# Decoder trunk on one core: one TensorE pass per gate entry issued in two pieces

## Chip, core and metric

The kernel runs on 1 core of one Trainium2 chip. The metric is the device time of the whole program in microseconds (us); lower is better.

## What is computed

The reference is a trunk of two layers (D_MODEL 1024, 256 tokens, D_FF 2816), each of three sub-layers: a SwiGLU feed-forward network (FFN), a token mixer, and a second FFN. So the program holds four FFNs, and the change touches only these.

```python
def swiglu(x, w_gate, w_up, w_down):
    return (jax.nn.silu(x @ w_gate) * (x @ w_up)) @ w_down
...
for l in range(DEPTH):
    f1 = swiglu(rms_norm(h, ffn1_pre_g[l]), ffn1_w_gate[l], ffn1_w_up[l], ffn1_w_down[l])
    h = h + 0.5 * rms_norm(f1, ffn1_post_g[l])
    m = token_mixer(rms_norm(h, mix_pre_g[l]), ...)
    h = h + rms_norm(m, mix_post_g[l])
    f2 = swiglu(rms_norm(h, ffn2_pre_g[l]), ffn2_w_gate[l], ffn2_w_up[l], ffn2_w_down[l])
    h = h + 0.5 * rms_norm(f2, ffn2_post_g[l])
```

## The kernel before

Every large product is done with each operand split into a high part and a low part (`fp32r`): three TensorE passes, high x high, high x low and low x high, add up in the same PSUM bank. A *pass* below is one `pe.matmul`; each comes with its own load of a 128 x 128 stationary operand (LDWEIGHTS, the engine row PEld), also where two passes in a row use the same one.

The 2816 hidden columns of an FFN are worked in 11 chunks of 256 (`NC` = 11; in the order strings they are 0 to 9 and A). Chunks 0 and 1 go by rows of tokens (`gu_rows`, passes of 512 columns). For chunks 2 to A, `gu_cols` computes the gate (step `G`, tile qg) and the up projection (step `U`, tile qu) with the hidden columns on the partitions: two halves `b` of 128 hidden columns, each 8 slices of K x 3 passes, so 48 passes of 256 columns (all 256 tokens) for one step. The stationary operand is a slice of the weight unit, the moving one is `xT`, the transposed tokens. `evac_cols` (step `E`) turns the two PSUM banks into the hidden tile `hT` on VectorE and ScalarE. `down` (steps `D`, c and token tile t) adds that chunk into four PSUM banks (facc): 2 token tiles x 2 halves of 512 output columns x 2 slices of K x 3 passes through `mm3` (L253, L254, L255), so 24 passes of 512 columns for the two steps of a chunk.

The order of TensorE's work is written out by hand:

```python
FFN_START = "g00 g10 sc0 xb1 u00 u10 e0 g01 g11 sc1 u01 u11 e1"
FFN_BODY = "G2 t0 rsb U2 t1 E2 side D00 D01 D10 D11 G3 U3 E3 D20 D21"
FFN_END = "D80 D90 DA0 fa0 D81 D91 fb0 xb0 DA1 fa1 fb1"
...
for c in range(4, NC):
    order += [f"{n}{c:X}" for n in "GUE"]
    if c < NC - 2:
        order += [f"D{c - 1:X}0", f"D{c - 1:X}1"]
```

So after G2 and U2, between which transposes stand (`t0`, `rsb`, `t1`: tiles ht and rsB), the steps run G3 U3 D2 G4 U4 D3 G5 U5 D4 G6 U6 D5 G7 U7 D6 G8 U8 D7 G9 U9 GA UA, then the downs of 8, 9 and A. Group c is entered through `down(1)` for c = 3, and through `down(c - 2)` for c = 4 to 9; group A follows U9 with no down step between. Weights stream from memory on SP's queue (`fetch`), are split by ScalarE (L229) and VectorE (L230) into ring units (`prepare`), and a unit is given back by `done` after the last pass that reads it.

Of the kernel before, what the change touches and what calls it, by code (L numbers as in the profile page):

```python
# [21 lines left out]
KD = D // P  # L22
S = 256
NT = S // P
# [20 lines left out]
FFN_BODY = "G2 t0 rsb U2 t1 E2 side D00 D01 D10 D11 G3 U3 E3 D20 D21"  # L45
FFN_END = "D80 D90 DA0 fa0 D81 D91 fb0 xb0 DA1 fa1 fb1"
NC = FF // 256

C_ID = 0
C_TRI = 128  # L50
# [36 lines left out]
def trunk(ctx: ExitStack, tc: tile.TileContext, T, out):  # L87
    nc = tc.nc
    pe, act, dve, pool = nc.tensor, nc.scalar, nc.vector, nc.gpsimd
# [13 lines left out]
    def bank(name):  # L103
        return psp.tile([P, 512], F32, tag="bank", name=name)

    def acc_tile(name):
        return [bank(name) for _ in range(2)]
# [13 lines left out]
    xT = big.tile([P, 2, KD, NT, P], F32R, name="xT")  # L121
# [18 lines left out]
    def cols_unit(key, W, k0, nk, c0, ncol):  # L140
        src = W[k0 * P:(k0 + nk) * P, c0:c0 + ncol].rearrange("(k p) c -> p k c", p=P)
        spec(key, [(0, P, nk, ncol, src)])

    def ffn_specs(l, f):
        wg, wu, wd = (T[f"ffn{f}_w_{n}"][l] for n in ("gate", "up", "down"))

        def gu(nm, c):
            cols_unit((l, f, nm, c), wg if nm == "g" else wu, 0, KD, c * 256, 256)

        def dn(c):  # L150
            cols_unit((l, f, "d", c), wd, 2 * c, 2, 0, D)

        for nm in "gu":
            for h in range(2):
                cols_unit((l, f, nm, h), wg if nm == "g" else wu, 4 * h, 4, 0, 512)
        for c in range(2, NC):
            gu("g", c)
            gu("u", c)
            if c == 2:
                dn(0)  # L160
                dn(1)
            elif c < NC - 1:
                dn(c - 1)
        dn(NC - 2)
        dn(NC - 1)

# [78 lines left out]
    def done(key, raw_only=False):  # L245
        del units[key]
        st["raw" if raw_only else "live"] -= 1
        pump()

    def mm3(o, pairs, first, last):  # L250
        n = len(pairs)
        for i, (sh, sl, mh, ml) in enumerate(pairs):
            pe.matmul(o, sh, mh, start=first and i == 0, stop=False)  # L253
            pe.matmul(o, sh, ml, start=False, stop=False)  # L254
            pe.matmul(o, sl, mh, start=False, stop=last and i == n - 1)  # L255


    def rstd(srcs, name, scale, eps=None):
# [70 lines left out]
    def ffn(l, f, rs, finish, side=None):  # L329
# [11 lines left out]
        def gu_rows(nm, h, t):  # L341
            if h == 0:
                ps[nm, t] = bank("p" + nm)
            u = units[l, f, nm, h]
            mm3(ps[nm, t], [(xT[:, 0, 4 * h + k, t, :], xT[:, 1, 4 * h + k, t, :], u[:, 0, k, :], u[:, 1, k, :])
                            for k in range(4)], h == 0, h == 1)
            if t == 1:
                done((l, f, nm, h))
# [24 lines left out]
        def gu_cols(nm, c):  # L373
            o = bank("q" + nm)
            u = units[l, f, nm, c]
            for b in range(2):
                bs = slice(b * P, (b + 1) * P)
                o3 = o[:, b * 256:(b + 1) * 256].rearrange("p (t n) -> p t n", t=NT)
                n = 0
                for k in range(KD):  # L380
                    for a, h in ((0, 0), (0, 1), (1, 0)):
                        pe.matmul(o3, u[:, a, k, bs], xT[:, h, k], start=n == 0, stop=n == 3 * KD - 1)  # L382
                        n += 1
            ps[nm] = o
            done((l, f, nm, c))
# [14 lines left out]
        def down(c, t):  # L400
            if acc[t] is None:
                acc[t] = acc_tile("facc")
            u = units[l, f, "d", c]
            if c < 2:
                q = [[hT[t][:, a, (2 * c + k) * P:(2 * c + k + 1) * P] for k in range(2)] for a in range(2)]
            else:
                q = [[hT["c", c][:, a, k * 256 + t * P:k * 256 + (t + 1) * P] for k in range(2)] for a in range(2)]
            for j, js in enumerate(HALF):
                mm3(acc[t][j], [(q[0][k], q[1][k], u[:, 0, k, js], u[:, 1, k, js]) for k in range(2)],
                    c == 0, c == NC - 1)  # L410
            if t == 1:
                done((l, f, "d", c))

        order = (FFN_FIRST if side else FFN_START).split() + FFN_BODY.split()
        for c in range(4, NC):
            order += [f"{n}{c:X}" for n in "GUE"]
# [3 lines left out]
        for n in order:  # L420
            if n == "rsb":
                tmp["rsB"] = broadcast_rows(rs)
            elif n == "side":
                if side:
                    side()
            elif n[:2] == "fa":
                finish[0](int(n[2]), acc[int(n[2])], ev[int(n[2])])
            elif n[:2] == "fb":
                finish[1](int(n[2]))
            elif n[:2] == "sc":  # L430
                scales(int(n[2]))
            elif n[:2] == "xb":
                if n[2] == "1" or not finish[2]:
                    pre_b(int(n[2]))
            elif n[0] in "gu":
                gu_rows(n[0], int(n[1]), int(n[2]))
            elif n[0] == "e":
                evac_rows(int(n[1]))
            elif n[0] == "t":
                tr(int(n[1]))  # L440
            elif n[0] in "GU":
                gu_cols(n[0].lower(), int(n[1], 16))
            elif n[0] == "E":
                evac_cols(int(n[1], 16))
            else:
                down(int(n[1], 16), int(n[2]))
# [85 lines left out]
    def mixer(l, rs, finish):  # L532
# [15 lines left out]
        def proj(nm, t):  # L548
            if nm == "kw":
                kwps[t] = o = bank("kw")[:, :280]  # L550
            else:
                accs[nm, t] = o = bank(nm)
            for h in range(2):
                u = units[l, nm, h]
                mm3(o, [(xT[:, 0, 4 * h + k, t, :], xT[:, 1, 4 * h + k, t, :], u[:, 0, k, :], u[:, 1, k, :])
                        for k in range(4)], h == 0, h == 1)
                if t == 1:
                    done((l, nm, h))
# [461 lines left out]
```

## Time and profile before

| | |
|---|---|
| median of 2 runs | 979.79 us (979.56 to 980.02) |
| profiled execution, whole time | 977.4 us |
| its span, first to last instruction | 975.4 us |
| TensorE passes / weight loads | 6294 / 6294 |
| TensorE busy | 956.4 us, 98% of the span |

The whole time of the profiled execution is 2.0 us above its span, and 2.4 us below the median. Busy time of TensorE overlaps from pass to pass, because a pass is shown from its start until its last result is written; the pace of a stream of passes is read from the distance of starts, or from the chain of work, which gives each pass only the time until the next one.

### The profile page before, as it was taken

To read this page: it belongs to the slowest core of one execution; us is meant where nothing else is said; L and a number is where in the kernel's file an instruction comes from. 1 tells how busy PE (TensorE), PEld (TensorE's weight loads), DVE (VectorE), ACT (ScalarE), POOL (GpSimd) and SP (SyncE) were. 2 spreads that over 40 slices of the span, in tenths; PEclk is the share of its full clock that TensorE was granted. 3 is DMA by queue.
4 is the path that set the end of the run, shared out by engine and by line. 5 is a ranking of instruction groups with operands and counts; after the bars stand their busy time and mean duration, and the time that the engine had idled before them with its cause. 6 is when DMAs were issued, how large, how long until landed. Compare 5 with 4: busy or idle time off the path is not lost.

```text
span 975.4 us, 15327 instructions
## 1 busy us (share of the span) xinstructions
PE 956.4 (98%) x6294; PEld 857.2 (88%) x6294; DVE 646.5 (66%) x864; ACT 478.7 (49%) x760; POOL 81.3 (8%) x136
## 2 busy tenths in 40 slices
PE   6999999999999999999999999999999999999997
PEld 5999999988778999999989999998887789999996
DVE  5785565678988655565677565567699777565552
ACT  5663443457557543443455443445468464443431
POOL 2000000030034000000030000003101320000000
PEclk9999999999999999999999999999999999999999
DMA  8876565457526555565557565653773167655611
GB/s 294 304 250 192 191 196 175 151 178 172 169 76 214 199 192 174 191 196 175 171 178 254 190 197 177 191 196 113 196 194 107 44 204 249 197 191 176 195 63 43
DMA packets 123294, 175.99 MB, mean 180 GB/s; under 512 B 13092, under 2 KB 95320, under 8 KB 123224
## 3 DMA queue, kind: packets, MB, share of 16 engines
q1 hardware_dynamic: 122936, 174.43, 56.1%
q8 instruction: 49, 0.80, 0.3%
q10 hardware_dynamic: 288, 0.59, 0.2%
q14 instruction: 21, 0.17, 0.1%
HBM read 173.95 MB, written 1.05 MB: 179 GB/s over the span
## 4 chain that ended last, share of the span: by engine, by line
PE 95%; DVE 2%; ACT 1%; DMA 1%; issue 0%; DVEq 0%; POOLq 0%; ACTq 0%; POOL 0%
PE qg L382 21%; PE qu L382 21%; PE facc L253 8%; PE facc L255 8%; PE facc L254 8%; PE oacc L253 2%; PE pu L255 2%; PE pu L253 2%; PE pg L254 1%; PE oacc L255 1%; PE pu L254 1%; PE oacc L254 1%; PE pg L255 1%; PE pg L253 1%; PE yT L767 1%; PE chp L795 1%
## 5 line engine op out<-in xcount | busy, mean ns | idle before, releaser
L229 ACT ACTIVATE unit<-raw 128x1024 fp32r<-128x1024 f32 (+2 forms) x320 | 322.5, 1033 | 348.0 <-issue 291.7
L230 DVE TENSOR_TENSOR unit<-raw,unit 128x1024 fp32r<-128x1024 f32 (+2 forms) x320 | 375.8, 1195 | 135.1 <-ACT unit L229 134.8
L382 PEld LDWEIGHTS qg<-xT,unit 128*128 128x128 f32 x1728 | 207.6, 189 | 2.5
L382 PE MATMUL qu<-xT,unit 128*128 128x256 f32 x1728 | 208.9, 281 | 0.0
L382 PE MATMUL qg<-xT,unit 128*128 128x256 f32 x1728 | 208.6, 280 | 0.0
L382 PEld LDWEIGHTS qu<-xT,unit 128*128 128x128 f32 x1728 | 205.4, 189 | 0.0
L253 PE MATMUL facc<-unit,hT 128*128 128x512 f32 x352 | 137.7, 391 | 0.0
L255 PE MATMUL facc<-unit,hT 128*128 128x512 f32 x352 | 137.0, 389 | 0.0
L254 PE MATMUL facc<-unit,hT 128*128 128x512 f32 x352 | 136.9, 389 | 0.0
L255 PEld LDWEIGHTS facc<-unit,hT 128*128 128x128 f32 x352 | 66.1, 188 | 13.8
L254 PEld LDWEIGHTS facc<-unit,hT 128*128 128x128 f32 x352 | 66.1, 188 | 12.4
L253 PEld LDWEIGHTS facc<-unit,hT 128*128 128x128 f32 x352 | 66.1, 188 | 12.4
L392 DVE TENSOR_TENSOR gp<-qg,rsB 128x512 f32<-128x512 f32 x36 | 24.8, 690 | 64.3 <-PE qg L382 64.3
L269 POOL TENSOR_TENSOR mspost<-ev,s 128x1 f32<-128x1 f32 x8 | 4.7, 592 | 664.2 <-ACT sq L263 664.2
L397 DVE SCALAR_TENSOR_TENSOR h<-qu,m 128x512 f32<-128x512 f32 x36 | 24.9, 691 | 50.8 <-PE qu L382 50.4
L394 ACT ACTIVATE m<-gp 128x512 f32<-128x512 f32 x36 | 22.3, 619 | 10.7 <-DVE gp L392 10.6
L743 ACT ACTIVATE pr<-s,mx 128x128 f32<-128x128 f32 (+1 forms) x64 | 26.1, 432 | 2.5 <-DVE mx L741 2.4
L395 DVE SCALAR_TENSOR_TENSOR m<-m,gp 128x512 f32<-128x512 f32 x36 | 24.7, 686 | 3.7 <-ACT m L394 3.7
L253 PE MATMUL pg<-unit,xT 128*128 128x512 f32 x64 | 26.0, 407 | 0.4 <-ACT unit L229 0.4
L293 DVE TENSOR_TENSOR fg<-facc,gpost 128x512 f32<-128x512 f32 x16 | 10.8, 688 | 23.5 <-ACT sq L263 23.5
L254 PE MATMUL pg<-unit,xT 128*128 128x512 f32 x64 | 25.9, 405 | 0.1
L255 PE MATMUL pg<-unit,xT 128*128 128x512 f32 x64 | 25.5, 399 | 0.0
(259 smaller groups left out, 1103.0 us busy)
## 6 DMA issues: line engine op xcount, KB each, us to landing
raw<-in_ffn_w_down_dram SPq DMA_DIRECT2D x44, 1024.0 KB, 5.0
raw<-in_ffn_w_gate_dram SPq DMA_DIRECT2D x42, 1024.0 KB, 5.4
raw<-in_ffn_w_up_dram SPq DMA_DIRECT2D x42, 1024.0 KB, 5.3
raw<-in_w_in_dram SPq DMA_DIRECT2D x14, 1024.0 KB, 5.4
raw<-in_w_out_dram SPq DMA_DIRECT2D x4, 1024.0 KB, 5.1
raw<-in_w_out_dram SPq DMA_DIRECT2D x8, 512.0 KB, 7.1
raw<-in_w_in_dram SPq DMA_DIRECT2D x4, 560.0 KB, 3.8
raw<-in_ffn_w_up_dram SPq DMA_DIRECT2D x4, 512.0 KB
```

Source lines behind the costliest of these rows:

```text
L229: act.activation(u[:, 0, i:i + step], r[:, i:i + step], AF.Copy)
L230: dve.tensor_sub(u[:, 1, i:i + step], r[:, i:i + step], u[:, 0, i:i + step].bitcast(F32))
L253: pe.matmul(o, sh, mh, start=first and i == 0, stop=False)
L254: pe.matmul(o, sh, ml, start=False, stop=False)
L255: pe.matmul(o, sl, mh, start=False, stop=last and i == n - 1)
L293: dve.tensor_mul(fg, acc[h], gpost[:, sl])
L382: pe.matmul(o3, u[:, a, k, bs], xT[:, h, k], start=n == 0, stop=n == 3 * KD - 1)
L392: dve.tensor_tensor(b2(gp), b2(g), tmp["rsB"][:, None, :].to_broadcast([P, 2, S]), op=ALU.mult)
L394: act.activation(m, gp, AF.Tanh, scale=0.5)
L395: dve.scalar_tensor_tensor(m, m, 1.0, gp, op0=ALU.add, op1=ALU.mult)
L397: dve.scalar_tensor_tensor(h, u, 0.5, m, op0=ALU.mult, op1=ALU.mult)
L743: act.activation(prs[v][:, b0 + i, :], sb[v][:, i, :], AF.Exp, bias=mx[:, i:i + 1], accum_out=cf[:, v, b0 + i:b0 + i + 1])
```

## The change

One pass next to the entry of each of the gate groups 3 to 9 is issued as two passes on column ranges of the same result, in one of three forms. For groups 3, 6 and 9 it is the first gate pass (256 columns), issued as two of 128, one for each token tile. For groups 4 and 7 it is the last pass of the down step before (512 columns, token tile 1, output half 1), issued as 256 + 256; for groups 5 and 8 the same pass as 384 + 128. The sums are the same. Nothing else moves. An FFN gets 7 more passes and weight loads, the program 28.

```diff
+ENTRY_G = (3, 6, 9)
+EXIT_D = {2: (256,), 5: (256,), 3: (384,), 6: (384,)}
...
-    def mm3(o, pairs, first, last):
+    def mm3(o, pairs, first, last, cut=()):
         n = len(pairs)
         for i, (sh, sl, mh, ml) in enumerate(pairs):
             pe.matmul(o, sh, mh, start=first and i == 0, stop=False)
             pe.matmul(o, sh, ml, start=False, stop=False)
-            pe.matmul(o, sl, mh, start=False, stop=last and i == n - 1)
+            if cut and i == n - 1:
+                for a, b in zip((0,) + cut, cut + (512,)):
+                    pe.matmul(o[:, a:b], sl, mh[:, a:b], start=False, stop=last, skip_group_check=True)
+            else:
+                pe.matmul(o, sl, mh, start=False, stop=last and i == n - 1)
...
-                        pe.matmul(o3, u[:, a, k, bs], xT[:, h, k], start=n == 0, stop=n == 3 * KD - 1)
+                        if n == 0 and b == 0 and nm == "g" and c in ENTRY_G:
+                            for t in range(NT):
+                                pe.matmul(o3[:, t], u[:, a, k, bs], xT[:, h, k, t], start=t == 0, stop=False,
+                                          skip_group_check=True)
+                        else:
+                            pe.matmul(o3, u[:, a, k, bs], xT[:, h, k], start=n == 0, stop=n == 3 * KD - 1,
+                                      skip_group_check=True)
                         n += 1
...
-                    c == 0, c == NC - 1)
+                    c == 0, c == NC - 1, EXIT_D.get(c, ()) if (t, j) == (1, 1) else ())
```

## Rows read from the trace of the kernel before

**Rows 1.** The page: busy time, granted clock by slices, chain by engine.

```profile
PE 956.4 (98%) x6294; PEld 857.2 (88%) x6294; DVE 646.5 (66%) x864; ACT 478.7 (49%) x760; POOL 81.3 (8%) x136
...
PEclk9999999999999999999999999999999999999999
...
PE 95%; DVE 2%; ACT 1%; DMA 1%; issue 0%; DVEq 0%; POOLq 0%; ACTq 0%; POOL 0%
```

**Rows 2.** Chain in order of time, group 5 (start us, us, what).

```profile
91.92 0.23 PE facc L254
92.15 0.23 PE facc L255
92.38 5.65 PE qg L382 x48
98.03 5.65 PE qu L382 x48
103.68 0.23 PE facc L253
```

**Rows 3.** Chain in order of time, group 2 of the last FFN.

```profile
806.77 0.24 PE pu L255
807.00 5.46 PE qg L382 x48
812.46 0.44 PE ht L369 x4
812.90 0.22 PE rsB L323 x2
813.12 5.46 PE qu L382 x48
818.58 0.44 PE ht L369 x4
```

**Rows 4.** Timeline inside qg, group 5, then group 2 (start, us, engine, instruction).

```profile
92.80 4.87 PE L382 MATMUL qg<-xT,unit 128*128 128x256 f32 x40
...
807.76 4.70 PE L382 MATMUL qg<-xT,unit 128*128 128x256 f32 x40
```

**Rows 5.** Groups by form inside the same two streams: busy us, mean ns.

```profile
L382 PE MATMUL qg<-xT,unit 128*128 128x256 f32 x40 | 4.9, 281 | 0.0
...
L382 PE MATMUL qg<-xT,unit 128*128 128x256 f32 x38 | 4.5, 276 | 0.0
```

**Rows 6.** Windows of group 5 (G, U, D4), then G2 of two FFNs.

```profile
core 0: us, PE busy (x) PEld busy (x) DVE busy (x) ACT busy (x) POOL busy (x), PEclk, DMA share, GB/s
92.21:97.87 5.66, 5.66 (x50) 5.65 (x49) 2.36 (x2) 2.01 (x2) 0.00 (x0) 1.00 0.70 201
97.87:103.52 5.65, 5.65 (x51) 5.65 (x49) 3.65 (x4) 2.53 (x3) 0.00 (x0) 1.00 0.64 184
103.52:108.96 5.44, 5.44 (x27) 4.51 (x25) 3.65 (x4) 2.53 (x3) 0.00 (x0) 1.00 0.46 180
514.58:520.05 5.47, 5.47 (x50) 5.47 (x49) 4.09 (x4) 2.01 (x2) 0.00 (x0) 1.00 1.01 344
806.84:812.30 5.46, 5.46 (x50) 5.46 (x48) 4.08 (x4) 2.01 (x2) 0.00 (x0) 1.00 1.04 357
```

**Rows 7.** Timeline, 24-pass streams of the two mixers, chp and chg.

```profile
251.49 3.09 PE L795 MATMUL chp<-xT,unit 128*128 128x256 f32 x24
...
257.96 3.07 PE L795 MATMUL chg<-xT,unit 128*128 128x256 f32 x24
...
730.12 3.01 PE L795 MATMUL chp<-xT,unit 128*128 128x256 f32 x24
...
736.51 2.98 PE L795 MATMUL chg<-xT,unit 128*128 128x256 f32 x24
```

**Rows 8.** Chain in order of time, group A after U9, second FFN.

```profile
457.67 5.65 PE qu L382 x48
463.32 5.65 PE qg L382 x48
468.98 5.65 PE qu L382 x48
```

**Rows 9.** Timeline of weight loads in front of short passes, second mixer.

```profile
744.04 0.98 PEld L690 LDWEIGHTS cs<-kk,qT 128*128 128x128 f32 x8
```

**Rows 10.** Window of D0 and D1 after U2, third FFN (columns as in Rows 6).

```profile
526.51:537.51 11.00, 11.00 (x51) 9.10 (x50) 6.50 (x7) 4.92 (x6) 0.00 (x0) 1.00 0.57 183
```

## The prediction

> **What bounds the kernel now.** I read the page first. TensorE is busy for 98% of the span, 95% of the chain that ended last runs through it, and the granted clock is in its top tenth in every slice, so the upper of the two levels, 2.4 GHz [rows 1]. There is no idle time to win: what counts is how long each TensorE pass takes until the next one starts. A mean over the kernel hides that, so I read the chain in order of time, stream by stream. A gate or up step of group 5 takes 5.65 us for its 48 passes, and the down passes around it 0.23 us each [rows 2]. The gate step of group 2, with the same 48 passes of the same shape, takes 5.46 us [rows 3]. This difference is the subject of the case.
>
> Inside the two streams the pace can be worked out from the timeline: (4.87 - 0.281) / 39 = 117.7 ns from start to start in group 5, and (4.70 - 0.276) / 39 = 113.4 ns in group 2 [rows 4], with the durations of one pass from the groups by form, 281 and 276 ns [rows 5]. So the same instruction has two paces, **loose** (117.7) and **tight** (113.4), and each stream keeps its own to the end. Half of the 512-column pace, 5.44 / 24 = 226.7 ns [rows 6], is 113.3 ns, so the tight pace is what the columns need and the loose one adds 4.3 ns to each pass.
>
> What decides between them? Not load from outside: the loose windows have less VectorE work and less DMA than the tight ones (DMA share 0.70 and 0.64 against 1.01 and 1.04) [rows 6]. Not shape or code line: in the mixers the same line runs 24 passes in 3.09 and 3.07 us in one layer and in 3.01 and 2.98 us in the other [rows 7]. What fits is **how the stream is entered**. Group 2's gate comes out of pu passes and its up step out of transposes: tight in all four FFNs (8 streams). Groups 3 to 9 are entered straight out of a down stream that runs at an even 226.7 ns; these gate steps, and the up steps right behind them, are all loose, and so are the gate and up steps of A, which follow U9 without a break and just keep the pace [rows 8]. That makes 8 groups x 2 steps x 4 FFNs = 64 loose streams of 48 passes, 3072 passes x 4.3 ns = 13.2 us, which is all that there is to win.
>
> **The change part by part.** The change puts a short pass into each of these 28 entries. First the cost, then what it may set off.
>
> *First gate pass as 128 + 128 (groups 3, 6, 9).* A pass can't start before its stationary operand is in. The streaming of 128 columns would take half of 113.4, 57 ns, but each piece brings a load of its own. In front of passes of 32 columns, eight such loads show a pace of (0.98 - 0.19) / 7 = 113 ns, with 0.19 us for one load [rows 9]; transposes of 128 columns run at 0.44 / 4 = 110 ns [rows 3]. No row shows an fp32r pass of 128 columns, so the cost of the extra piece lies between 0 (two pieces of 57 ns) and 118 ns (two at the loose pace in place of one). I take the load as what binds, the nearest rows: 2 x 110 - 116 = 104 ns. Twelve of them: 1.25 us, bounds 0 to 1.4.
>
> *Last down pass as 256 + 256 (groups 4, 7).* Two tight passes are 227 ns, what the whole pass takes; two loose ones are 235.4, 9 ns more. Eight of them: 0 to 0.07 us, I take 0.03.
>
> *Last down pass as 384 + 128 (groups 5, 8).* The 384 columns lie midway between 113.4 and 226.7, so 170 ns, then 110 for the piece that waits for its load: 280 - 227 = 53 ns. Eight of them: 0.42 us, bounds 0 to 0.45.
>
> All pieces lie on the path, since TensorE has no gap in which they could hide. **Sum of the costs: 1.7 us, bounds 0 to 1.9.** No DMA, no other engine's instruction and no queue is moved; the bank given to the next step and the unit given back by `done` are signalled by the last piece, at most a tenth of a us later. VectorE is busy for 2.4 to 3.7 us of a step of 5.65 us [rows 6], so it also keeps up with steps that are 0.2 us shorter.
>
> *What it may set off.* A stream that turns tight at its entry saves 5.65 - 5.46 = 0.19 us in the gate step, settling included [rows 2, 3], and 48 x 4.3 ns = 0.21 us in each step behind it that keeps the pace. That is 0.40 us for a group, and 0.82 us for the entry of group 9, which carries A too. Over four FFNs: the 128 + 128 entries (3, 6, 9) can give 4 x (0.40 + 0.40 + 0.82) = 6.5 us, the 384 + 128 entries (5, 8) 3.2 us, the 256 + 256 entries (4, 7) 3.2 us, 12.9 us in all.
>
> *What is given back.* A down stream that comes out of a tight up step may need some passes to come back to 226.7 ns. The one case of before is D0 and D1 behind U2: 11.00 us against 2 x 5.44 = 10.88 [rows 6, 10], most of which is the step out of the transposes. I take 0.03 us for each down step behind a group that turned tight, and 0 to 0.06 (passes at 229 in place of 226.7 ns) as bounds.
>
> *Which forms work?* The 128-column pieces make TensorE wait for a weight load, as nothing in the even down stream does; entries behind short passes and transposes are those that are mostly tight in before (all U2; of the four mixer streams shown, two) [rows 3, 7]. 256 + 256 leaves no such wait: the gate is then entered out of 256-column passes, and in before U entered from a loose G stays loose [rows 2, 8]. So I expect the two forms with a 128-column piece to work and 256 + 256 not to.
>
> [...]
>
> **The rivals.**
>
> A (forecast): the 20 entries with a 128-column piece turn tight, the 8 others stay loose. -6.5 - 3.2 + 1.7 + 0.6 (20 down or closing steps at 0.03) = -7.4 us, so 977.4 - 7.4 = 970.0 in a profiled execution, or 979.8 - 7.4 = 972.4 as a median (the median is 2.4 us above the profiled time).
>
> B: all 28 turn tight; any disturbance next to the entry is enough. -12.9 + 1.7 + 0.8 = -10.4, so 969.4. For it: the pu stream ahead of G2 has passes of 512 columns only, and still leads to tight [rows 3]. Against it: what is said of 256 + 256.
>
> C: only one of the forms with a 128-column piece works. 128 + 128 alone: -6.5 + 1.7 + 0.4 = -4.4, so 975.4. 384 + 128 alone: -3.2 + 1.7 + 0.2 = -1.3, so 978.5.
>
> D, on the other side (slower than before): the pace is set by something that the short pass doesn't touch, such as the operands of the stream itself, each entry falls back to 117.7 ns, and only the costs are left: +1.7, so 981.5; up to +3.6 (983.4) if 28 down steps lose their even pace as well, at 0.06 each. It decides as soon as fewer than about 5 entries turn: 1.7 us of cost over 0.40 of gain is four to five. For it: down to gate is loose in 28 of 28 cases, so this state is a strong one, and mixer streams behind short passes are loose too [rows 7].
>
> That the change doesn't do what it says would be 28 pieces that the compiler joins again, with no difference; the count of passes, 6322 in place of 6294, would tell.
>
> **How the numbers follow.** A 0.35, B 0.27, C 0.15, D 0.20, others (a costlier piece, or no pieces) 0.03. The forecast is A: 972.4, and with the costs open by about 2 us either way I keep 972.4. The range reaches from B with a part of its cost bounds (968) over A and C to D's first value (982): it leaves out the lowest part of B, the upper part of D and the others, under 2 in 10. A measurement of this kernel can tell 2% (19.6 us) from no change by the bound used here; the most that could be won is 13.2 us and no sum of costs reaches 5, so within 2% has 0.98, and each side 0.01.
>
> **What the profile of the changed kernel would show.** TensorE stays at 98% with no idle before it, and 28 more passes. For each group the chain gives G and U as 5.65 (loose) or about 5.46 (tight); that says form by form which entries turned. In G3, G6 and G9 the first two passes would be about 110 ns apart if the load binds, 57 if only the columns count. Down steps at 5.44 us say that nothing is given back, 5.5 that the even pace is lost. I am wrong if the 256 + 256 entries turn, if a 128-column entry stays at 117.7, or if a stream that starts tight falls back before its 48 passes end.

## The result and the profile after

The changed kernel takes 968.0 us (median of 2 runs, 967.9 to 968.11) against 979.79 before: -11.8 us, ratio 0.988 with a 95% interval of 0.9837 to 0.9922. So it is faster, by more than the runs vary, and by less than 2%. The forecast was 972.4 with a range of 968 to 982, so the time lies on the low edge of the range, and the forecast missed by 4.4 us. What came is the outcome of rival B, all 28 entries turned, and not case A: the range reached down to 968 only to take in B, so that the time falls inside it is luck as far as A goes, and no support for its mechanism.

The page's busy row, which answers to the one in [rows 1]: 28 more passes and loads, TensorE still at 98% of a span that is 9.2 us shorter.

```profile
span 966.2 us, 15383 instructions
...
PE 947.4 (98%) x6322; PEld 847.4 (88%) x6322; DVE 646.8 (67%) x864; ACT 478.5 (50%) x760; POOL 81.3 (8%) x136
```

The chain in order of time through groups 4, 5 and 6 and then A of the first FFN; it answers to [rows 2]. In the changed kernel L260 is the split down pass, L391 the split gate pass, L394 the whole gate and up passes.

```profile
75.30 0.23 PE facc L260 x2
75.53 5.46 PE qg L394 x48
80.99 5.44 PE qu L394 x48
...
91.89 5.51 PE qg L394 x48
97.40 5.44 PE qu L394 x48
...
108.30 0.17 PE qg L391 x2
108.47 5.39 PE qg L394 x47
113.86 5.44 PE qu L394 x48
...
168.52 5.44 PE qg L394 x48
173.96 5.44 PE qu L394 x48
```

Read the second column. Each up step is at 5.44 us in place of 5.65, and so are GA and UA (the rows at 168.52 and 173.96); the same holds in all four FFNs. The gate step tells the price of its form: 5.46 us behind 256 + 256, 5.51 behind 384 + 128, and 0.17 + 5.39 = 5.56 with 128 + 128. Both pieces of the down pass together take 0.23 us, like the whole pass in [rows 2].

The pace inside the gate of group 5, in the timeline and the groups by form, and the window of the down step that follows a tight up step (D3; columns: length, then busy us of PE, PEld, DVE, ACT, POOL, granted clock, DMA share, GB/s):

```profile
92.82 4.36 PE L394 MATMUL qg<-xT,unit 128*128 128x256 f32 x37
```

```profile
L394 PE MATMUL qg<-xT,unit 128*128 128x256 f32 x37 | 4.4, 277 | 0.0
...
86.27:91.73 5.46, 5.46 (x28) 4.55 (x26) 3.66 (x4) 2.53 (x3) 0.00 (x0) 1.00 0.53 190
```

(4.36 - 0.277) / 36 = 113.4 ns from start to start, the pace of group 2 in [rows 4]. The down step takes 5.46 us against 5.44 in [rows 6]: 0.02 us is given back.

**The sum.** Per FFN the gates win 3 x 0.09 + 2 x 0.19 + 2 x 0.14 + 0.21 (A) = 1.14 us and eight up steps 8 x 0.21 = 1.68; six down steps give back 6 x 0.02 = 0.12. That is 2.7 us, 10.8 over four FFNs, from rounded rows; read off the chain from the start of G3 to the end of UA, each FFN takes 120.33 us in place of 123.09, so 11.0 over four. The two profiled times differ by 977.4 - 968.1 = 9.3 us only. Most of the rest lies in the second mixer, in windows of the changed kernel in which the granted clock isn't 1.00, and in the chain through them (yT, then cs):

```profile
730.00:733.00 3.00, 2.00 (x17) 1.52 (x15) 2.87 (x9) 2.81 (x6) 0.00 (x0) 1.00 0.04 14
733.00:736.00 3.00, 2.98 (x8) 0.88 (x10) 3.00 (x5) 2.51 (x5) 0.00 (x0) 0.79 0.00 0
736.00:739.00 3.00, 3.00 (x17) 1.71 (x15) 0.56 (x3) 0.63 (x1) 0.00 (x0) 0.64 0.68 207
...
734.14 3.01 PE yT L780 x8
...
737.37 1.30 PE cs L703 x8
```

The same pieces of the chain of before, at a granted clock of 1.00:

```profile
742.24 1.87 PE yT L767 x8
...
744.27 0.87 PE cs L690 x8
```

(3.01 - 1.87) + (1.30 - 0.87) = 1.6 us on these pieces. In the changed kernel G3 of the first FFN also starts 0.2 us later (59.07 us against 58.88), and 11.0 - 1.6 - 0.2 = 9.2 is what the spans differ by. In the 13 runs of the kernel before that stand beside e1 to e4, those with a mean granted clock of 0.999 took 977.1 to 977.8 us and those with 0.997 or less 979.3 us and more; the profiled execution of before (977.4, clock 0.999) is one of the first kind and the changed one (968.1, clock 0.997) one of the second, so the medians, 11.8 us apart, and the chain's 11.0 describe the change better than 9.3.

### The profile page after: what moved, and what is told of

It is laid out like the page before. It is cut to its first block, busy times and chain, and to the rows that moved or that the text cites. A ratio compares the mean times of both kernels' runs of the same rounds, so it can differ in the third digit from the quotient of the medians.

```text
span 966.2 us, 15383 instructions
## 1 busy us (share of the span) xinstructions
PE 947.4 (98%) x6322; PEld 847.4 (88%) x6322; DVE 646.8 (67%) x864; ACT 478.5 (50%) x760; POOL 81.3 (8%) x136
## 4 chain that ended last, share of the span: by engine, by line
PE 93%; DVE 2%; ACT 2%; DMA 1%; issue 0%; DVEq 0%; POOLq 0%; ACTq 0%; POOL 0%; SPq 0%
PE qg L394 20%; PE qu L394 20%; PE facc L256 8%; PE facc L257 8%; PE facc L262 8%; PE oacc L256 2%; PE pu L256 2%; PE pg L257 2%; PE pu L262 2%; PE oacc L262 2%; PE oacc L257 2%; PE pu L257 2%; PE pg L262 1%; PE pg L256 1%; PE yT L780 1%; PE xt L320 1%
## 5 line engine op out<-in xcount | busy, mean ns | idle before, releaser
L394 PE MATMUL qu<-xT,unit 128*128 128x256 f32 x1728 | 202.1, 277 | 0.0
L394 PE MATMUL qg<-xT,unit 128*128 128x256 f32 x1716 | 201.9, 277 | 0.0
L394 PEld LDWEIGHTS qu<-xT,unit 128*128 128x128 f32 x1728 | 198.6, 188 | 0.0
L394 PEld LDWEIGHTS qg<-xT,unit 128*128 128x128 f32 x1716 | 198.0, 188 | 0.3
L256 PE MATMUL facc<-unit,hT 128*128 128x512 f32 x352 | 137.9, 392 | 0.0
L257 PE MATMUL facc<-unit,hT 128*128 128x512 f32 x352 | 137.3, 390 | 0.0
L262 PE MATMUL facc<-unit,hT 128*128 128x512 f32 x336 | 131.1, 390 | 0.0
L256 PEld LDWEIGHTS facc<-unit,hT 128*128 128x128 f32 x352 | 66.1, 188 | 12.5
L257 PEld LDWEIGHTS facc<-unit,hT 128*128 128x128 f32 x352 | 66.1, 188 | 12.5
L262 PEld LDWEIGHTS facc<-unit,hT 128*128 128x128 f32 x336 | 63.1, 188 | 13.3
L300 DVE TENSOR_TENSOR fg<-facc,gpost 128x512 f32<-128x512 f32 x16 | 10.8, 689 | 23.5 <-ACT sq L270 23.5
```

Of the source, the lines that this page charges most:

```text
L300: dve.tensor_mul(fg, acc[h], gpost[:, sl])
```

## The experiments

Two theories at the start. *Entry state*: the pace is a state of the pass stream; an even down stream of 512-column passes hands over the loose one, a short pass beside the gate's first passes turns it, and it then holds until the next down step. *Rivals*: one disturbance serves a whole FFN; each group needs its own form; a piece must make TensorE wait for its weight load; the operands, not the timing, set the pace. All kernels below start from the changed one, with the two tables edited as shown.

**One form at a time.**

```diff
-ENTRY_G = (3, 6, 9)
-EXIT_D = {2: (256,), 5: (256,), 3: (384,), 6: (384,)}
+# e1_tok369: ENTRY_G = (3, 6, 9);             EXIT_D = {}
+# e2_all256: ENTRY_G = ();                    EXIT_D = {c: (256,) for c in 1..7}
+# e3_all384: ENTRY_G = ();                    EXIT_D = {c: (384,) for c in 1..7}
+# e4_alltok: ENTRY_G = (3, 4, 5, 6, 7, 8, 9); EXIT_D = {}
```

> The 128 + 128 entries of groups 3, 6 and 9 alone; groups 4, 5, 7 and 8 are entered out of whole passes as before. Entry theory (the down stream comes back to its even 226.7 ns and brings each new gate back to the loose 117.7 ns): groups 3, 6, 9 and A tight, the others loose at 5.65 us a step; per FFN 3 x 0.095 + 5 x 0.213 - 2 x 0.02 = 1.3 us, so 5.2 us below the kernel before. Rival (one disturbance turns the whole rest of an FFN): all groups from 3 on are tight, some 12 us below.

Measured: 974.86 us (10 runs) against 979.45 for 13 runs of the kernel before, -4.6; ratio 0.9954 (0.9938 to 0.9971). Chain in order of time, groups 3 to 6:

```profile
59.54 0.17 PE qg L391 x2
59.71 5.39 PE qg L394 x47
65.10 5.44 PE qu L394 x48
76.00 5.65 PE qg L394 x48
81.65 5.65 PE qu L394 x48
92.74 5.65 PE qg L394 x48
98.40 5.65 PE qu L394 x48
109.49 0.17 PE qg L391 x2
109.66 5.39 PE qg L394 x47
115.05 5.44 PE qu L394 x48
```

Group 3 is tight, 4 and 5 are loose again, 6 is tight. One down step of 24 whole passes undoes the turn, so every entry needs its own split. The rival of one disturbance per FFN is out.

> All seven entries by 256 + 256 in the last down pass. Entry theory, with the prices read from the changed kernel's trace (gate step 5.46 us, up step 5.44 us, down step 5.46 us): per FFN 6 x (0.195 + 0.213) + 0.195 + 3 x 0.213 - 7 x 0.02 = 3.1 us, so 12.6 us below the kernel before and 1.5 us below the changed one. Rival (a 128-column piece that waits for its load is needed at least in some groups, and groups 4 and 7 profit from the groups ahead of them): groups 3, 5, 6, 8, 9 stay at 5.65 us, and no more than 3 us is won.

Measured: 967.07 us (4 runs), -12.4 against the same 979.45; ratio 0.9877 (0.9854 to 0.9901). Group 3 in the chain, as all later groups:

```profile
59.44 0.23 PE facc L260 x2
59.67 5.46 PE qg L394 x48
65.13 5.44 PE qu L394 x48
```

All entries turn with the form that I had expected not to work. It costs nothing beyond the 0.02 us in the gate step and the 0.02 in the down step. By these rows a FFN wins 6 x (0.19 + 0.21) + 0.19 + 3 x 0.21 - 6 x 0.02 = 3.1 us, 12.4 in all, and this is the best version that I found: 1.6 us below the changed kernel by the chain (119.94 us against 120.33 from G3 to UA), while the two ratios (0.9877 and 0.988) have intervals that overlap.

> All seven entries by 384 + 128 in the last down pass. Entry theory: all tight, gate step 5.51 us; per FFN 6 x (0.14 + 0.213) + 0.14 + 3 x 0.213 - 7 x 0.02 = 2.8 us, so 11.1 us below the kernel before, 1.5 us above the version with 256 + 256 everywhere. Rival (the form has to fit the group): some groups stay at 5.65 us.

Measured: 967.61 us (4 runs), -11.8; ratio 0.9886 (0.9862 to 0.991). All gates at 5.51, all up steps at 5.44 us.

> All seven entries by 128 + 128 in the first gate pass. Entry theory: all tight, gate step 5.56 us; per FFN 6 x (0.095 + 0.213) + 0.095 + 3 x 0.213 - 7 x 0.02 = 2.4 us, so 9.7 us below the kernel before, the smallest gain of the three forms. Rival (the form has to fit the group): some groups stay at 5.65 us.

Measured: 969.84 us (4 runs), -9.6; ratio 0.9902 (0.9881 to 0.9923). All gates at 0.17 + 5.39, all up steps at 5.44 us. The forms come out in the order of their prices in the chain: 256 + 256, 384 + 128, 128 + 128. No group is tied to a form.

**Where the split must be.** In e5 the split sits in the first of the 24 down passes (and the last is whole again), in e6 at the 25th of the 48 gate passes:

```diff
# e5_first_down256, in mm3 and down
+            if cut and i == 0:
+                for a, b in zip((0,) + cut, cut + (512,)):
+                    pe.matmul(o[:, a:b], sh, mh[:, a:b], start=first and a == 0, stop=False, skip_group_check=True)
...
-                    ... if (t, j) == (1, 1) else ())
+                    ... if (t, j) == (0, 0) else ())
# e6_mid_gate, in gu_cols, with ENTRY_G = (3, 4, 5, 6, 7, 8, 9)
-                        if n == 0 and b == 0 and nm == "g" and c in ENTRY_G:
+                        if n == 0 and b == 1 and nm == "g" and c in ENTRY_G:
```

> The same 256 + 256 split, and the same number of passes, but in the first of the 24 passes of the down step (token tile 0, half 0) in place of the last. Entry theory: 23 whole passes bring the down stream back to 226.7 ns, so the gate is entered as before: gate and up steps 5.65 us, the whole 0 to 1 us above the kernel before. Rival (the number of passes, or any split in the down step, decides): gate 5.46 and up 5.44 us, some 12 us below.

Measured: one run, 978.32 us, and in the chain

```profile
59.07 5.65 PE qg L394 x48
64.73 5.65 PE qu L394 x48
```

Loose in every group: the same number of passes and loads as in e2, 23 passes earlier, wins nothing. The count of passes is not what turns the stream.

> The 128 + 128 split in the middle of the gate step (first pass of its second half, the 25th of 48) for groups 3 to 9. If the pace is a state of the stream that a short pass can turn anywhere: the first 24 passes at 117.7 ns, the rest at 113.4, gate step 2.83 + 2.72 + 0.12 = 5.67 us, up step 5.44 us, A tight; per FFN 9 x 0.213 - wait costs of 7 x 0.04 = about 1.4 us for the steps U3 to U9, GA and UA, so 5.5 to 7 us below the kernel before. Rival (only the crossing from the down stream can set it, because the state goes with the operands that change there): gate 5.65 + 0.12 = 5.77, up 5.65 us, 3 us above.

Measured: one run, 970.34 us at a mean granted clock of 0.999, 7.1 us below the profiled execution of before at the same clock; in the chain

```profile
58.99 2.83 PE qg L394 x24
61.82 0.17 PE qg L391 x2
61.99 2.67 PE qg L394 x23
64.66 5.44 PE qu L394 x48
```

24 passes at 2.83 / 24 = 118 ns, then the split, then 23 at an average of 116 with the settling in it, and an up step at 5.44 us. A loose stream can be turned in its middle, so the crossing from down to gate is not needed; it is only the earliest place.

**How short the piece may be.** EXIT_D for c = 1 to 7 with (496,), (480,), (448,) and, with the short piece first, (128,):

> All seven entries by 496 + 16 columns in the last down pass: a piece that streams in no time, so that only the extra weight load is left. If the extra load ahead of the gate (the wait for it) turns the pace: all tight, gate step about 5.5 us, 10 to 12 us below the kernel before. Rival (the columns of the last whole piece must be 256 or a multiple of 128 for the phase to change): gate and up stay at 5.65 us, and the pieces cost 28 x 0.1 = 3 us.

Measured: one run, 980.56 us. Chain of group 4:

```profile
75.61 5.75 PE qg L394 x48
81.37 5.65 PE qu L394 x48
```

The gate step pays 0.10 us over 5.65, which I take for the wait for the load, and stays loose, in all 28 groups. This is the run that takes the expected trigger apart: a wait for a weight load at the entry is not enough.

> All seven entries by 448 + 64 in the last down pass, between 384 + 128 (which turned every entry) and 496 + 16 (which turned none). If the extra load and the wait for it were enough, 496 + 16 would have turned too, so the length of the piece counts. Theory of a length threshold: no figure for where it lies; at 64 columns either all gates are tight (gate step about 5.6 us, some 9 us below the kernel before) or all loose (5.74 us, 3 us above). Rival (each group decides for itself): a mixture over the groups.

Measured: one run, 966.58 us. All groups tight:

```profile
75.07 5.54 PE qg L394 x48
80.60 5.44 PE qu L394 x48
```

> All seven entries by 128 + 384 in the last down pass: the short piece first, so that the gate is entered behind a piece of 384 columns that hides its load. If the short pass must be the one next to the gate: loose, gate 5.65 us, about 1 to 3 us above the kernel before. If any break in the even row of whole passes right ahead of the gate is enough: tight, gate about 5.5 us, 10 to 12 us below.

Measured: one run, 968.38 us. All groups tight:

```profile
75.11 0.29 PE facc L260 x2
75.39 5.46 PE qg L394 x48
```

Here the wait falls between the two pieces (0.29 us in place of 0.23) and the gate is entered without one, behind 384 columns.

> All seven entries by 480 + 32 in the last down pass, between 448 + 64 (all gates tight, gate step 5.54 us) and 496 + 16 (all loose, 5.76 us). Both the tight and the loose outcome are open; what is tested is whether all groups again go the same way, as a state that the length of the piece sets for every entry alike would have it (tight: about 5.57 us a gate step and some 9 us below the kernel before; loose: 5.74 us and 3 us above), or whether groups differ, as chance at the entry would have it.

Measured: one run, 969.78 us. All groups tight, the gate step shown here for group 4:

```profile
75.87 5.56 PE qg L394 x48
81.43 5.44 PE qu L394 x48
```

It pays the same 0.10 us over its pace as 496 + 16, and turns. So a last piece of 32 columns or more turned all 28 entries, one of 16 none, and at each size all groups went the same way. Each of these four sizes or orders has one execution.

**Timing or operands.** No split; in `gu_cols` the three passes of a K slice in another order:

```diff
-                    for a, h in ((0, 0), (0, 1), (1, 0)):
+                    for a, h in ((0, 0), (1, 0), (0, 1)):
```

> No split anywhere; in gate and up steps the three passes of a K slice run as high x high, low x high, high x low (weights x tokens), so that the stationary operands alternate in another order while the lengths of all passes stay. If the pace is a matter of timing at the entry alone, nothing changes: gate and up 5.65 us, same time as before. Rival (the operands of neighbouring passes set it): another pace in all 64 streams, 5.44 us if the conflict is gone (13 us below the kernel before), or more than 5.65.

Measured: 979.4 us (10 runs), ratio 1.0002 (0.9989 to 1.0015), and the loose gate of before, here of group 3:

```profile
59.85 5.65 PE qg L394 x48
```

At these entries the other order changes nothing, as a matter of timing would have it. It is one other order, within the gate and up steps; the operands of the down steps were left as they are.

**Not every entry is settled by its form.** G2 and U2, which no edit here splits (e10's order holds for them too), come out of pu passes and of transposes, and in the profiled execution of before all eight are tight. In those of e1 and e2 one of the eight, U2 of the first FFN, is loose, and in that of e10 G2 of the first FFN (5.66 us). U2 in before, then in e2:

```profile
41.52 5.46 PE qu L382 x48
```

```profile
42.12 5.66 PE qu L394 x48
```

The transposes in front are the same and the granted clock is 1.00 in both. So an entry of this kind can go either way, in code that e1 and e2 leave as it is, while in all 14 profiled executions every gate step of groups 3 to 9 that was entered out of whole passes, without a split, was loose, and those with the same split went alike.

**The same for the row streams.** On top of e2, a split in the gate and up passes of chunks 0 and 1, whose 512-column passes run at 229 ns:

```diff
-                            for k in range(4)], h == 0, h == 1)
+                            for k in range(4)], h == 0, h == 1, (256,) if h == 0 else ())
```

> 256 + 256 at all seven entries, as before, and also in the last pass of the first half of K of each gate and up step of chunks 0 and 1 (four per FFN), whose streams run at 229 ns in place of 226.7 (16 more splits). If these streams can be turned like the others: 96 passes per FFN at 226.7 ns, 0.2 us per FFN and 0.8 us in all below the version with 256 + 256 at the entries alone; their 24-pass steps take 5.44 us. Rival (this pace belongs to the operands of these streams and comes back within a few passes): their steps stay at 5.49 us and the splits cost 16 x 0.02 = 0.3 us.

Measured: 967.71 us (4 runs), ratio 0.9881 (0.9858 to 0.9904), no gain over e2. Windows of one 24-pass step, of before and then of this run (25 passes):

```profile
317.45:322.95 5.50, 5.50 (x26) 4.51 (x24) 2.21 (x3) 2.01 (x2) 0.00 (x0) 1.00 0.02 4
```

```profile
316.83:322.33 5.50, 5.50 (x26) 4.55 (x25) 2.20 (x3) 2.01 (x2) 0.00 (x0) 1.00 0.01 1
```

The step keeps its 5.50 us, one pass more included. Behind the split the whole passes start 226 to 232 ns apart at once, as before, so one short pass doesn't turn this pace for good; why these streams differ was not tested.

## Why the prediction came out as it did

*What bounds the kernel*: right. TensorE has no gap before or after, and all of the gain is pace: 5.65 to 5.44 us in each up step. That a stream keeps its pace to the end, and hands it on from U9 to GA and UA, held too.

*Price of 128 + 128*: 104 ns were expected on top of a tight gate step of 5.46 us, and 5.56 - 5.46 = 0.10 us came. The size was right, but its sign was not: the two pieces start 60 ns apart, near the 57 that were to mean that only the columns count, the first whole pass 109 ns behind the second piece, and the next one 172 ns behind that in place of 113, so half of the price is paid by a whole pass. The weight loads in this stretch start 108 and 111 ns apart, near the 110 and 113 ns of [rows 3] and [rows 9], so the load is still the likely bound. *384 + 128*: 53 ns expected; 5.51 - 5.46 = 0.05 us came. *256 + 256*: 0 to 9 ns expected; nothing shows, 0.23 us for both pieces. *Given back by the down steps*: 0.03 us expected, 0.02 came. The sum of costs was right: 12 x 0.10 + 8 x 0.05 = 1.6 us against 1.7. B was worked out at 969.4; the median is 968.0.

*Which forms work*: this step failed, and with it the choice of A over B; the prediction named it as a sign of being wrong (the 256 + 256 entries turn). I took the wait for a weight load as what turns the stream, and so expected 256 + 256 to fail. It works in all groups (e2), without any wait; and 496 + 16 has the wait and works in none (e7). What was taken from U2, tight in all four FFNs, came from one execution: in those of e1 and e2 one U2 behind the same transposes is loose. The argument from U steps that stay loose behind a loose gate was also no evidence: there the stream enters in the loose state, and nothing disturbs it; between a down step at its even pace and a gate, one 256-column pass does. What the runs put in its place: any split tried whose pieces have 32 columns or more, in the last pass before the gate or inside the gate stream, turns it (e2, e3, e4, e6, e8, e9, e12). Nor does B's reason hold as it stands, that any disturbance next to the entry is enough: 496 + 16 is one, and turns nothing.

*Rival D* (only costs) is what happens when the split has a piece too short (e7) or too far from the gate (e5): 5.65 us steps and the price of the pieces.

*The Trainium skill*, "TensorE: Matmul & The Clock Gate", section "Back-to-back issue gap", gives N / 2.4 + 2.5 ns as the gap of an isolated pass with the clock warm, and says that in a stream of weight loads and passes both set the spacing. The trace here adds that even the sizes of both don't fix it: e2 and e5 have the same passes and loads of the same sizes, one split moved by 23 places, and their gate passes run at 113 and at 118 ns.

**Left open.** Shown is that the pace is a state that a split pass can turn and that 24 whole down passes undo (e1), and that it didn't depend on the operands' order in the one other order tried. Which part of the hardware holds this state (the spacing of weight loads against the moving stream is one candidate) was not tested, nor why the limit lies between 16 and 32 columns. The single records have a mark of it: in the loose streams read in before, e7 and e10, every third weight load takes 192 ns and the others 187 or 188, in either order of the operands, while in the tight streams read in before and e2 all take 187 or 188 once the pace has settled. That shows where to look, and not what comes first.

## What to carry to other kernels

Where TensorE has no gaps left, compare the chain's time per step among steps of identical passes: a step that is a few per cent longer than its twin, pass by pass, may be in another state, as here, and what stands in front of it is the place to look. Then try to split one pass next to the entry into two halves; here 256 + 256 cost 0.02 us and won 0.4 us for a gate and up pair. The split had to be repeated behind each down step of 24 whole passes.

## What was not expected of the hardware

One instruction form, with the same operands and the granted clock at 1.00, ran at two steady paces, 113.4 and 117.7 ns, the loose one over up to 192 passes in a row. Behind a down step, one pass split in two decided which; the turn takes some passes, as the starts of the first five gate passes behind 256 + 256 lie 114 to 121 ns apart before they settle at 113.

In the second mixer of the changed kernel the granted clock showed 0.79 and 0.64 in two windows of 3 us, behind a window in which TensorE was busy for 2.00 of 3 us. At 1.2 GHz, the lower of the two levels, for part of that time, one group of eight passes took 3.01 us in place of 1.87. In the profiled execution of before the clock stayed at 1.00 at that place, behind a window with TensorE busy for 2.09 of 3 us, so what sets off the fall is not shown. It cost 1.6 us, as much as all the splits together. It doesn't go by the number of splits: between 735 and 750 us the granted clock was 0.89 in e2 and 1.00 in e3, which have the same count of passes.
